# A batched matrix product on one core: the first x load divided between two issuing engines

## The chip, the core and the metric

The kernel runs on one core of a Trainium2 chip. The metric is the device time of one execution in microseconds (us); lower is better. Where a profile is quoted, its times are those of one profiled execution, counted from the start of its span. PE is TensorE, DVE is VectorE, ACT is ScalarE, POOL is GpSimd and SP is SyncE; a q behind the name (SPq) means the sequencer of that engine, which issues DMAs and waits on semaphores. Data moves between the chip's memory (HBM) and the on-chip buffers by 16 DMA engines, which all issuing engines share.

## The reference

128 independent products of a 256 x 512 matrix with a 512 x 384 matrix, all in float32:

```python
b1, b2, m, k, n = 8, 16, 256, 512, 384
x      = randn(b1, b2, m, k)      # 67.1 MB
weight = randn(b1, b2, k, n)      # 100.7 MB
out    = np.matmul(x, weight)     # 50.3 MB, float32
```

## The kernel before

**Tiling.** The 128 products are taken in 32 groups of G = 4 (the text calls a group n). A group's x is 1024 rows of 512 numbers, 2 MB: partition p holds eight rows that follow one another in memory, 16 KB (`x_sb`, two buffers). Its weights are 3 MB (`w_sb`, two buffers), and its result is 1.5 MB (`out_sb`, four slots). The first four groups and the last two load their weights in two pieces of 1.5 MB each, with 12 KB to a partition; the others in one piece with 24 KB to a partition.

**Stages of a group.** Each has T = 4 quarters.
- SyncE loads x (`load_x`, line 121) and the weights (`load_w`, line 138), and stores the result (`store`, line 160). Each load and store is one DMA, or two for weights in pieces. GpSimd makes the identity matrix for the transposes at the start, and stores one group late in the run (`store_rest`).
- VectorE casts x to bf16 (`cast_x`, line 194, four casts a group) and most of the weights (`cast_w`, line 207; `cast_short`, line 223, for the groups with divided weights). ScalarE casts the other weights (line 207).
- TensorE transposes x through PSUM (line 247), two bf16 numbers as one float32 word. ScalarE evacuates the transposed x to `x_t` (`evacuate`, line 234).
- TensorE multiplies (line 265; line 283 for the last group). ScalarE copies the products out of PSUM (`copy_out`, line 300).

**What sets the order.** The order is written out by hand: each engine has its own program (`on_sync`, `on_vector`, `on_tensor`, `on_scalar`, `on_gpsimd`), and semaphores that only count up tie them together. SyncE issues x and weights of group 0, then of group 1; x of group 2 has to wait until the four casts of group 0 have freed `x_sb0` (`x_cast`), and weights of group 2 until the weights of group 0 are cast (`w_vcast`, `w_acast`). In the loop it issues, per group, a load of x, a store of the group four before, and a load of weights. All DMAs that SyncE issues stand in one hardware queue, in that order. VectorE casts x of group 0 first, then per group its weights and x of the next group. ScalarE is one group ahead with its evacuations.

**Around the change.** SyncE's program starts with `load_x(e, 0, NG, 0)`, a DMA of 2 MB to 128 partitions that counts 16 on `x_in0` when it has landed. VectorE's first cast waits for that count. ScalarE's program starts with four increments (lines 385 to 388), which set the counters `t_copied`, `o_copied` and the two `o_out` to their starting values, and then evacuates group 0 (line 405); up to there it issues no DMA.

Of the kernel before, what the change touches and what calls it, by code (L numbers as in the profile page):

```python
# [12 lines left out]
def kernel(  # L13
# [7 lines left out]
    P = 128  # L21

    b1, b2, M, K = x.shape
# [4 lines left out]
    x_rows = x.rearrange("b1 b2 m k -> (b1 b2 m) k")  # L28
# [12 lines left out]
    G = 4  # L41
    C = P // G
    R = G * M // P
# [22 lines left out]
    def sbuf(name, shape, dtype, n):  # L66
        return [
            ctx.enter_context(nc.sbuf_tensor(f"{name}{s}", shape, dtype)) for s in range(n)
        ]
# [6 lines left out]
    def sems(name, n):  # L76
        return [tc.alloc_semaphore(f"{name}{s}") for s in range(n)]
# [3 lines left out]
    x_sb = sbuf("x_sb", [P, R, K], fp32, XS)  # L81
# [19 lines left out]
    x_in, w_in, o_out = sems("x_in", XS), sems("w_in", WS), sems("o_out", 2)  # L101
    h_in = sems("h_in", G)
    o_end = sems("o_end", 1)[0]
    rest_out = sems("rest_out", 1)[0]
    o_fin, spare = sems("o_fin", 1)[0], sems("spare", 1)[0]


# [2 lines left out]

    def load_x(e, t, U, s):
        n = t * U + s
        if not isinstance(n, int) or n >= XS:
            e.wait_ge(x_cast, n * T + (1 - XS) * T)
        rows = x_rows[bass.ds(n * (G * M), G * M)]
        if is_full(n):
            src = rows.rearrange("(i p r) k -> p i r k", i=G, p=P)
            dst = x_sb[s % XS][:].rearrange("p (i r) k -> p i r k", i=G)
        else:
            src, dst = rows.rearrange("(p r) k -> p r k", r=R), x_sb[s % XS][:]  # L120
        e.dma_start(dst, src).then_inc(x_in[s % XS], 16)  # L121

    def is_short(n):
        return isinstance(n, int) and (n < LAG or n >= NG - 2)

    def is_full(n):
        return isinstance(n, int) and n == NG - 1

    def load_w(e, t, U, s):
        n = t * U + s  # L130
        if not isinstance(n, int) or n >= WS:
            e.wait_ge(w_vcast, n * CV + (1 - WS) * CV)
            e.wait_ge(w_acast, n * CA + (1 - WS) * CA)  # L133
        d = SL // SH if is_short(n) else 1
        k = SL * KO // d
        for h in range(d):
            sem = h_in[s % WS * 2 + h] if is_short(n) else w_in[s % WS]
            e.dma_start(  # L138
                w_sb[s % WS][:, h * k : (h + 1) * k, :],
                w_rows[bass.ds(n * (G * K) + h * (G // d * K), G // d * K)].rearrange(  # L140
                    "(p k) n -> p k n", k=k
                ),
            ).then_inc(sem, 16)

    def store(e, t, U, s, pieces=1):
        n = t * U + s
        dram = o_rows[bass.ds(n * (G * M), G * M)].rearrange("(p r) n -> p r n", r=R)
        if is_full(n):
            dram = o_rows[n * G * M : (n + 1) * G * M].rearrange("(i p r) n -> p i r n", i=G, p=P)
        for q in range(pieces):  # L150
            rows = slice(q * R // pieces, (q + 1) * R // pieces)
            last = isinstance(n, int) and n >= NG - OS
            if not last and (not isinstance(n, int) or n >= 2):
                e.wait_ge(o_out[s % 2], (t * (U // 2) + s // 2) * 16 + 16)
            e.wait_ge(o_copied, n * T + ((q + 1) * T // pieces + BIAS))
            src = out_sb[:, bass.ds(slot(t, U, s) * R + q * R // pieces, R // pieces)]
            if is_full(n):
                src = src.rearrange("p (i r) n -> p i r n", i=G)
                rows = slice(0, G)
            e.dma_start(out=dram[:, rows], in_=src).then_inc(  # L160
                o_fin if last and n == NG - 1 else o_end if last else o_out[s % 2], 16
            )
# [24 lines left out]
    def cast_x(e, t, U, s, q):  # L187
        n = t * U + s
        if q == 0:
            e.wait_ge(x_in[s % XS], (t * (U // XS) + s // XS) * 16 + 16)  # L190
        e.wait_ge(t_made, n * T + (q + 1 - T + BIAS))  # L191
        rows = slice(2 * q, 2 * q + 2)
        S = SH if is_short(n) else SL
        e.tensor_copy(  # L194
            out=x_bf[s % BS][:, rows].rearrange("p r (s q c) -> p r s q c", s=S, c=KO),
            in_=x_sb[s % XS][:, rows].rearrange("p r (q s c) -> p r s q c", s=S, c=KO),
        ).then_inc(x_cast, 1)

    def cast_w(e, t, U, s, parts, first=True):
        n = t * U + s  # L200
        if first:
            e.wait_ge(p_made, n * T + (BIAS - T))
            e.wait_ge(w_in[s % WS], (t * (U // WS) + (s - LAG) // WS) * 16 + 16)  # L203
        copy = e.tensor_copy if e is nc.vector else e.copy
        for c in parts:
            i, h = c // SL, c % SL
            copy(  # L207
                out=w_bf[(s * G + i) % WBS][h * C : (h + 1) * C],
                in_=w_sb[s % WS][i * C : (i + 1) * C, h * KO : (h + 1) * KO, :],
            ).then_inc(w_vcast if c < CV else w_acast, 1)  # L210
# [17 lines left out]
    def evacuate(e, t, U, s, parts=range(T)):  # L228
        n = t * U + s
        if parts[0] == 0:  # L230
            e.wait_ge(p_made, n * T + (BIAS - T))
        for q in parts:
            e.wait_ge(t_made, n * T + (q + 1 + BIAS))
            e.copy(  # L234
                out=x_t[s % TS][:, 2 * q : 2 * q + 2],
                in_=pt[(s * T + q) % PT][:].bitcast(bf16),
            ).then_inc(t_copied, 1)
# [54 lines left out]
    def copy_out(e, t, U, s, q):  # L292
        n = t * U + s
        if q == 0:
            if isinstance(n, int) and is_shared(n - OS):
                e.wait_ge(rest_out, 16 * 3)
            elif not isinstance(n, int) or n >= OS:
                e.wait_ge(o_out[s % 2], (t * (U // 2) + s // 2) * 16 + (16 - OS // 2 * 16 + 16))
        e.wait_ge(p_made, n * T + (q + 1 + BIAS))
        e.copy(  # L300
            out=out_sb[:, bass.ds(slot(t, U, s) * R + 2 * q, 2), :],
            in_=po[(s * T + q) % PO][:, :, :N],
        ).then_inc(o_copied, 1)
# [10 lines left out]
    def on_sync(e):  # L314
        U = 2
        for n in range(LAG):
            load_x(e, 0, NG, n)
            load_w(e, 0, NG, n)
        rounds = (NG - 2 - LAG) // U
        with e.Fori(0, rounds) as t:  # L320
            for s in range(U):
                load_x(e, t, U, LAG + s)
                store(e, t, U, s)
                load_w(e, t, U, LAG + s)

        for n in range(LAG + rounds * U, NG):
            load_x(e, 0, NG, n)
            load_w(e, 0, NG, n)
        for n in range(NG - 1 - LAG, NG):
            store(e, 0, NG, n)  # L330
        e.wait_ge(o_end, 16 * (OS - 1))
        with e.Fori(0, 4):
            e.sem_inc(spare, 1)
        for _ in range(PAD):
            e.sem_inc(spare, 1)
        e.wait_ge(o_fin, 16)
# [45 lines left out]

    def on_scalar(e):
        U = 2
        e.sem_inc(t_copied, BIAS)
        e.sem_inc(o_copied, BIAS)
        for s in range(2):
            e.sem_inc(o_out[s], 16)

        def step(t, U, s):
            short = is_short(t * U + s + 1)
            evacuate(e, t, U, s + 1, range(T - 1))
            for q in range(T):
                copy_out(e, t, U, s, q)
                if q == 0:
                    evacuate(e, t, U, s + 1, range(T - 1, T))
                if q == 0 and short:
                    e.sem_inc(w_acast, CA)  # L400
                if q > 0 and not short:
                    last = CA if q == T - 1 else q
                    cast_w(e, t, U, s + 1, range(CV + q - 1, CV + last), q == 1)

        evacuate(e, 0, NG, 0)
        e.sem_inc(w_acast, CA)
        for n in range(LAG - 1):
            step(0, NG, n)
        rounds = (NG - 2 - LAG) // U
        with e.Fori(0, rounds) as t:  # L410
            for s in range(LAG - 1, LAG - 1 + U):
                step(t, U, s)
        for n in range(LAG - 1 + rounds * U, NG - 1):
            step(0, NG, n)
        for q in range(T):
            copy_out(e, 0, NG, NG - 1, q)
# [3 lines left out]
    on_vector(nc.vector)  # L420
    on_tensor(nc.tensor)
    on_scalar(nc.scalar)


# [28 lines left out]
```

## Time and profile before

| | |
|---|---|
| median of 3 runs | 515.99 us (515.84 to 516.26) |
| profiled execution | 516.01 us, of which its span is 514.2 us |
| instructions | 11664 |
| HBM read, written | 167.77 MB, 50.33 MB |
| rate over the span | 424 GB/s |
| DMA queue of SyncE (q1) | 216.54 MB, 98.8% of 16 engines' span |
| DMA queue of GpSimd (q0) | 1.57 MB, 0.7% |
| busy: PE, DVE, ACT, POOL | 62%, 77%, 80%, 1% of the span |
| the x loads | 32 of 2048 KB, median 22.3 us from issue to landing |
| the first x load | 2048 KB, issued at 0.90 us, 7.7 us from issue to landing |
| first cast of VectorE | starts at 8.65 us |
| first work of ScalarE | starts at 10.63 us |

The profile gives busy time by engine, the span in 40 equal slices (each digit is a busy share in tenths; GB/s is what the DMA engines moved), the DMA queues, the chain of work that ended last, and groups of instructions by line with what ended the idle time before them. Busy shares are averages over the whole span. The time from issue to landing of a DMA holds the time that it stands in its queue behind earlier ones. The trace behind the profile also has a record of every DMA packet, with its start, its length, its size and its queue; a packet here is one row of one partition, 16 KB of an x load, 12 or 24 KB of a weight load. A time share of the DMA engines can read a little over 1 in a narrow window, because a packet counts in the window in which it starts.

### The profile page before, as it was taken

Reading aid. Unit: us, or ns where it says so; the run is one execution under the profiler, and the core shown is the slowest. Engines: PE = TensorE matmul, PEld = TensorE weight load, DVE = VectorE, ACT = ScalarE, POOL = GpSimd, SP = SyncE. Lnnn points to the kernel's source line nnn. Section 1 sums busy time; section 2 is a strip of 40 time slices with the busy share of each in tenths; the row PEclk is TensorE's granted clock in tenths of the full one; section 3 lists DMA queues with packets and bytes.
Section 4 is the critical chain, followed back from the end, with each engine's and each line's share of the span. In section 5 each row is a group of like instructions: output and inputs, shape, how many; then the busy total and the mean of one; then the engine's idle time right before and its main releaser. Section 6 shows DMA issues by size and latency. Waiting matters only on the chain.

```text
span 514.2 us, 11664 instructions
## 1 busy us (share of the span) xinstructions
PE 316.8 (62%) x4512; PEld 222.5 (43%) x4512; DVE 397.6 (77%) x462; ACT 409.5 (80%) x387; POOL 3.7 (1%) x9
## 2 busy tenths in 40 slices
PE   2277837556675575866568656567545676474782
PEld 2255525434454343544435534345434354353551
DVE  2788757798777887778977779777798777887980
ACT  1365576997898989789978989987998798989752
POOL 0000000000000000000000000000000000010000
PEclk9687785877787778668776868886878787778887
DMA  8999999999999999999999999999999999999997
GB/s 334 429 427 422 438 423 427 436 430 435 420 427 433 433 436 429 425 429 433 440 427 428 427 435 429 438 426 426 431 437 435 425 426 429 435 435 420 422 426 308
DMA packets 15686, 218.18 MB, mean 424 GB/s; under 512 B 1728, under 2 KB 1728, under 8 KB 3008
## 3 DMA queue, kind: packets, MB, share of 16 engines
q1 hardware_dynamic: 15312, 216.54, 98.8%
q0 software_dynamic: 368, 1.57, 0.7%
q8 instruction: 3, 0.05, 0.0%
q14 instruction: 3, 0.02, 0.0%
HBM read 167.77 MB, written 50.33 MB: 424 GB/s over the span
## 4 chain that ended last, share of the span: by engine, by line
DMA 55%; DVE 31%; issue 9%; PE 1%; DVEq 1%; SPq 1%; ACT 0%; POOLq 0%
DMA w_sb<-in_weight_dram 55%; DVE w_bf L207 20%; DVE w_bf L223 5%; DVE x_bf L194 5%; PE po L283 1%; SPq L138 0%; DVEq L360 0%; SPq L121 0%; DVEq L64 0%; DVEq L203 0%; ACT out_sb L300 0%; SPq L133 0%; DVEq L191 0%; DVEq L217 0%; SPq L448 0%
## 5 line engine op out<-in xcount | busy, mean ns | idle before, releaser
L207 DVE CAST w_bf<-w_sb 32x1536 bf16<-32x1536 f32 x286 | 271.9, 951 | 81.9 <-DMA w_sb<-in_weight_dram 70.7
L265 PE MATMUL po<-w_bf,x_t 128*32 128x384 bf16 x3968 | 197.1, 358 | 34.1 <-DVE w_bf L207 29.5
L247 PE MATMUL pt<-identity,x_bf 128*128 128x128 f32 x512 | 114.7, 414 | 153.5 <-DVE x_bf L194 153.5
L207 ACT CAST w_bf<-w_sb 32x1536 bf16<-32x1536 f32 x130 | 190.9, 1468 | 5.5 <-DMA w_sb<-in_weight_dram 2.3
L247 PEld LDWEIGHTS pt<-identity,x_bf 128*128 128x128 f32 x512 | 103.4, 224 | 165.4 <-issue 165.1
L265 PEld LDWEIGHTS po<-w_bf,x_t 128*32 128x32 bf16 x3968 | 116.1, 105 | 113.8 <-issue 53.0
L300 ACT COPY out_sb<-po 128x768 f32 (+1 forms) x128 | 102.5, 801 | 58.8 <-PE po L265 54.7
L234 ACT COPY x_t<-pt 128x1024 bf16<-128x1024 bf16 x128 | 123.6, 1020 | 21.2 <-PE pt L247 20.6
L194 DVE CAST x_bf<-x_sb 128x1024 bf16<-128x1024 f32 x128 | 79.9, 688 | 12.3 <-DMA x_sb<-in_x_dram 11.5
L223 DVE CAST w_bf<-w_sb 64x1536 bf16<-64x1536 f32 x48 | 45.8, 955 | 7.4 <-DMA w_sb<-in_weight_dram 6.0
L234 ACT ACT_TABLE_LOAD x1 | 1.3, 1283 | 10.6 <-PE pt L247 10.6
L174 POOL DMA_DIRECT2D out_dram<-out_sb x3 | 3.1, 1020 | 458.9 <-DMA out_dram<-out_sb 458.9
L283 PE MATMUL po<-w_bf,x_t 128*128 128x384 bf16 x32 | 5.4, 326 | 0.4 <-DVE w_bf L223 0.4
L283 PEld LDWEIGHTS po<-w_bf,x_t 128*128 128x128 bf16 x32 | 3.1, 98 | 2.7 <-issue 0.7
masks.py:199 POOL TENSOR_SCALAR_AFFINE_SELECT identity<-identity 128x128 f32<-128x128 f32 x1 | 0.3, 283 | 0.2 <-POOL identity L306 0.2
L306 POOL MEMSET identity<- 128x128 f32 x1 | 0.2, 204 | 0.5 <-POOLq L64 0.5
L437 POOL MEMSET const-bfloat16-1.0<- 128x1 bf16 x1 | 0.1, 96 | 0.0
L437 POOL MEMSET const-uint8-127<- 128x1 uint8 x1 | 0.1, 96 | 0.0
L437 POOL MEMSET const-float32-0.0<- 128x1 f32 x1 | 0.1, 93 | 0.3 <-issue 0.3
L437 POOL MEMSET const-float32-1.0<- 128x1 f32 x1 | 0.1, 93 | 0.0
## 6 DMA issues: line engine op xcount, KB each, us to landing
w_sb<-in_weight_dram SPq DMA_DIRECT2D x26, 3072.0 KB, 18.1
x_sb<-in_x_dram SPq DMA_DIRECT2D x32, 2048.0 KB, 22.3
out_dram<-out_sb SPq DMA_DIRECT2D x31, 1536.0 KB, 25.0
w_sb<-in_weight_dram SPq DMA_DIRECT2D x12, 1536.0 KB, 16.7
out_dram<-out_sb POOLq DMA_DIRECT2D x1, 1440.0 KB, 16.8
out_dram<-out_sb POOLq DMA_DIRECT2D x1, 60.0 KB, 7.1
out_dram<-out_sb POOLq DMA_DIRECT2D x1, 36.0 KB, 17.6
```

The lines of the kernel that those rows point to most:

```text
L174: e.dma_start(out=dram[p : p + k], in_=out_sb[p : p + k, a : a + R], max_dma_last_dim=R // 2 * N * 4,).then_inc(rest_out, 16)
L194: e.tensor_copy(out=x_bf[s % BS][:, rows].rearrange("p r (s q c) -> p r s q c", s=S, c=KO), in_=x_sb[s % XS][:, rows].rearrange("p r (q s ...
L207: copy(out=w_bf[(s * G + i) % WBS][h * C : (h + 1) * C], in_=w_sb[s % WS][i * C : (i + 1) * C, h * KO : (h + 1) * KO, :],).then_inc(w_vcas ...
L223: e.tensor_copy(out=w_bf[(n * G + d * SH + a) % WBS][h * p : (h + 1) * p], in_=w_sb[n % WS][a * p : (a + 1) * p, r : r + KO, :],).then_inc ...
L234: e.copy(out=x_t[s % TS][:, 2 * q : 2 * q + 2], in_=pt[(s * T + q) % PT][:].bitcast(bf16),).then_inc(t_copied, 1)
L247: ins = e.transpose(pt[(s * T + q) % PT][:, rr, h, :], words[:, 2 * q + rr, h :: KO // 2], identity[:],)
L265: ins = e.matmul(po[(s * T + q) % PO][mine, rr, :N], x_t[s % TS][:, 2 * q + rr, ko // 2, mine, ko % 2], w_bf[(s * G + i) % WBS][:, ko, :], ...
L283: ins = e.matmul(po[(s * T + q) % PO][:, rr, :N], x_t[s % TS][:, 2 * q + rr, ko // 2, :, ko % 2], w_bf[(s * G + q) % WBS][:, ko, :], start ...
L300: e.copy(out=out_sb[:, bass.ds(slot(t, U, s) * R + 2 * q, 2), :], in_=po[(s * T + q) % PO][:, :, :N],).then_inc(o_copied, 1)
L306: e.memset(identity[:], 0.0).then_inc(id_done, 1)
L437: nc = _bacc.Bacc("TRN2", target_bir_lowering=False, num_devices=1)
```

## The change

The first load of x is divided by partitions. SyncE's DMA for group 0 now fills partitions 0 to 63 only, and counts on `x_in0` as before. ScalarE issues a DMA of its own for partitions 64 to 127, as the first instruction of its program, ahead of the four increments; it goes into ScalarE's own hardware queue and counts on a new semaphore, `x_half0`. VectorE's first cast of group 0 waits for both counts. The bytes and the layout in memory and on the chip are the same, and all later loads are as they were. In the built program ScalarE has one instruction more (the DMA), and the other engines have as many as before; VectorE's additional wait stands on a semaphore instruction that was already there.

```diff
--- before.py
+++ after.py
@@ -102,6 +102,7 @@
     h_in = sems("h_in", G)
     o_end = sems("o_end", 1)[0]
     rest_out = sems("rest_out", 1)[0]
+    x_half = sems("x_half", 1)[0]
     o_fin, spare = sems("o_fin", 1)[0], sems("spare", 1)[0]
 
 
@@ -113,12 +114,18 @@
         if not isinstance(n, int) or n >= XS:
             e.wait_ge(x_cast, n * T + (1 - XS) * T)
         rows = x_rows[bass.ds(n * (G * M), G * M)]
+        if isinstance(n, int) and n == 0:
+            return load_first(e, slice(0, P // 2), x_in[0])
         if is_full(n):
             src = rows.rearrange("(i p r) k -> p i r k", i=G, p=P)
             dst = x_sb[s % XS][:].rearrange("p (i r) k -> p i r k", i=G)
         else:
             src, dst = rows.rearrange("(p r) k -> p r k", r=R), x_sb[s % XS][:]
         e.dma_start(dst, src).then_inc(x_in[s % XS], 16)
+
+    def load_first(e, part, sem):
+        rows = x_rows[: G * M].rearrange("(p r) k -> p r k", r=R)
+        e.dma_start(x_sb[0][part], rows[part]).then_inc(sem, 16)
 
     def is_short(n):
         return isinstance(n, int) and (n < LAG or n >= NG - 2)
@@ -188,6 +195,8 @@
         n = t * U + s
         if q == 0:
             e.wait_ge(x_in[s % XS], (t * (U // XS) + s // XS) * 16 + 16)
+            if isinstance(n, int) and n == 0:
+                e.wait_ge(x_half, 16)
         e.wait_ge(t_made, n * T + (q + 1 - T + BIAS))
         rows = slice(2 * q, 2 * q + 2)
         S = SH if is_short(n) else SL
@@ -382,6 +391,7 @@
 
     def on_scalar(e):
         U = 2
+        load_first(e, slice(P // 2, P), x_half)
         e.sem_inc(t_copied, BIAS)
         e.sem_inc(o_copied, BIAS)
         for s in range(2):
```

## The prediction

> **What bounds the kernel now.** I read the page first: busy slices, the DMA queues, then the chain that ended last. After that I cut the start and the end of the span into narrow windows, and read the waits of VectorE in the first 30 us.
>
> The slices and queues on the page of the kernel before:
>
> ```profile
> DVE  2788757798777887778977779777798777887980
> ACT  1365576997898989789978989987998798989752
> DMA  8999999999999999999999999999999999999997
> GB/s 334 429 427 422 438 423 427 436 430 435 420 427 433 433 436 429 425 429 433 440 427 428 427 435 429 438 426 426 431 437 435 425 426 429 435 435 420 422 426 308
> q1 hardware_dynamic: 15312, 216.54, 98.8%
> DMA 55%; DVE 31%; issue 9%; PE 1%; DVEq 1%; SPq 1%; ACT 0%; POOLq 0%
> ```
>
> No compute engine is full in any long stretch. The 16 DMA engines are: SyncE's one queue occupies them for 98.8% of the span, and all slices but the first and the last lie between 420 and 440 GB/s. The chain's 55% on w_sb loads is mostly time in which a load stands in that queue behind others. So the time is what a pipe costs that is filled once, runs full, and is emptied once; only the first and the last slice have anything to give.
>
> Those two ends in windows (columns: stretch, its length, busy time by engine with counts, clock, DMA share, GB/s):
>
> ```profile
> 0.00:1.90 1.90, 0.00 (x0) 0.00 (x0) 0.00 (x0) 0.00 (x0) 0.69 (x6) 1.00 0.00 0
> 1.90:3.00 1.10, 0.00 (x0) 0.00 (x0) 0.00 (x0) 0.00 (x0) 0.00 (x0) 1.00 1.11 223
> 3.00:4.00 1.00, 0.00 (x0) 0.00 (x0) 0.00 (x0) 0.00 (x0) 0.00 (x0) 1.00 0.79 262
> 4.00:8.00 4.00, 0.00 (x0) 0.00 (x0) 0.00 (x0) 0.00 (x0) 0.00 (x0) 1.00 1.00 428
> ...
> 506.00:506.70 0.70, 0.00 (x0) 0.00 (x0) 0.00 (x0) 0.00 (x0) 0.00 (x0) 1.00 0.82 347
> 506.70:510.00 3.30, 0.00 (x0) 0.00 (x0) 0.00 (x0) 0.00 (x0) 0.00 (x0) 0.61 0.99 399
> 510.00:511.00 1.00, 0.00 (x0) 0.00 (x0) 0.00 (x0) 0.00 (x0) 0.00 (x0) 0.50 0.75 298
> 511.00:512.60 1.60, 0.00 (x0) 0.00 (x0) 0.00 (x0) 0.00 (x0) 0.00 (x0) 0.50 0.23 88
> 512.60:514.20 1.60, 0.00 (x0) 0.00 (x0) 0.00 (x0) 0.00 (x0) 0.00 (x0) 0.50 0.00 0
> ```
>
> The first packet starts at 1.92, 1.02 after SyncE's issue at 0.90. From 1.90 to 4.00 the engines move 223 x 1.10 + 262 x 1.00 = 507 KB, which at 428 GB/s is 1.18 us of work: the ramp wastes 2.10 - 1.18 = 0.92 us. Then the rate is full. The account closes: 218.18 MB at 428 GB/s is 509.8, and 1.90 + 0.92 + 509.8 = 512.6, where the last packet ends; 1.6 us of closing waits and barriers make 514.2. At the end most DMA engines finish by 511, a few at 511 to 512.6, so the slowest of them sets the end.
>
> How the start feeds VectorE, and what SyncE does meanwhile (start, duration, instructions, idle time before):
>
> ```profile
> 0.90 0.39 SPq L121 DMA_DIRECT2D x_sb<-in_x_dram  x1
> 1.35 0.89 SPq L138 DMA_DIRECT2D w_sb<-in_weight_dram  x2
> 2.28 0.64 SPq L121 DMA_DIRECT2D x_sb<-in_x_dram  x1
> 2.97 0.99 SPq L138 DMA_DIRECT2D w_sb<-in_weight_dram  x2
> ...
> 8.65 2.50 DVE L194 CAST x_bf<-x_sb 128x1024 bf16<-128x1024 f32 x4 [8.65 <-DMA x_sb<-in_x_dram]
> 12.41 3.91 DVE L223 CAST w_bf<-w_sb 64x1536 bf16<-64x1536 f32 x4 [1.26 <-DMA w_sb<-in_weight_dram]
> 17.22 3.91 DVE L223 CAST w_bf<-w_sb 64x1536 bf16<-64x1536 f32 x4 [0.90 <-DMA w_sb<-in_weight_dram]
> 22.13 2.50 DVE L194 CAST x_bf<-x_sb 128x1024 bf16<-128x1024 f32 x4 [0.99 <-DMA x_sb<-in_x_dram]
> 25.91 4.90 DVE L223 CAST w_bf<-w_sb 64x1536 bf16<-64x1536 f32 x5 [1.28 <-DMA w_sb<-in_weight_dram]
> ```
>
> By 3.96 SyncE has put 10.5 MB into its queue, 24.5 us of work, so the pipe can't run dry early. VectorE waits for a load four more times by 25.91, together 1.26 + 0.90 + 0.99 + 1.28 = 4.43 us.
>
> **The change part by part.** The sum is made against the profiled execution: 516.01, of which 514.2 is span and 1.8 lies around it. The median shown is 515.99, so the two stand as one.
>
> SyncE's issue of the first half. The instruction stays; it took 0.39. If its time goes with the bytes it takes about 0.20, and the six loads behind it move up to 0.19 earlier; if it goes with the number of DMA engines, nothing moves. Either way the queue already holds work when each DMA engine comes to it, so this is worth 0.
>
> ScalarE's issue. A new instruction at about 0.90, where ScalarE's first semaphore increment stands now. The nearest row is SyncE's issue at the same moment, 0.39 us. Behind it on ScalarE stand four semaphore increments (they end at 1.14 now, so 1.53 then) and the first evacuation. The increments release nobody early: TensorE's first transpose is at 9.45, the first store is issued at 37.98. ScalarE itself first has work at 10.63. Cost 0, with 8 us of cover.
>
> [...] No run shows a divided load yet.
>
> The bytes and their ends. The same 2 MB in the same 128 rows of 16 KB, 64 + 64, and 64 rows divide over 16 engines as evenly as 128. A second completion adds one 4-byte packet per DMA engine, which the packet records give as 9 ns: +0.01.
>
> VectorE's wait. One more semaphore before the first cast; a semaphore wait on VectorE is 0.02 us. What is queued behind it is all of VectorE's work, and SyncE's third x load waits for the four casts. The halves share the engines, so the later half lands about when the whole load did, 8.6. If an engine took all of SyncE's first weight piece before the second half, it would land later by 8 packets of 460 ns, 3.7 us. Less than the 4.43 us that VectorE waits anyway by 25.91; the third x load (11.18 now) has until about 27 before the queue runs dry. A later landing costs 0, an earlier one gains 0: the pipe is full.
>
> The ramp. This is the one unknown. Gain at most: 0.92, the whole waste, if two queues keep twice the reads under way while the first are slow. Loss: the packet records show the 16 DMA engines starting their first packet between 1.92 and 3.00, a spread of 1.08 within one DMA; if a second DMA's pushes come between the first's, the last engine starts up to 1.08 later. First packets took 0.61 to 1.76, later ones 0.61, so a second slow start costs one engine at most 1.15. The nearest row with two queues at once is GpSimd's store late in the run (queue q0 beside q1):
>
> ```profile
> 462.00:480.00 18.00, 10.71 (x152) 7.97 (x150) 14.51 (x17) 17.64 (x18) 1.71 (x2) 0.78 1.00 423
> 480.00:500.00 20.00, 15.46 (x277) 10.46 (x277) 18.66 (x22) 11.71 (x14) 0.00 (x0) 0.91 1.01 424
> ```
>
> With two queues 423 GB/s, with one 424, and the 16 KB packets still took 611 ns: sharing neither helps nor hurts. I take 0 for the ramp and keep -0.92 and +1.15.
>
> Sum: 0 + 0 + 0.01 + 0.02 (hidden) + 0 = 516.0. All of it is below 0.2% (1.03 us), which is about what a measurement of this kernel can tell from no change.
>
> **The rivals.**
>
> Faster: the ramp shrinks. For it: the ramp is the only idle stretch at the start, and each DMA engine would find two queues filled at once. Against it: the records show each engine working on one packet at a time, and the slow first packets end in two clusters near 3.1 and 3.7 whatever their start, as if the memory side held them. Half of the waste gives 515.5, all of it 515.1. Even that is within 0.2%; to pass 1.03 the first packets would also have to start 0.11 earlier.
>
> Slower: the two issues share one maker of descriptors. SyncE's pushes for engine after engine then alternate with ScalarE's, the spread of first starts grows from 1.08 to 2.16, and the engine that starts last is late by 1.08. As the engines run full to the end, the slowest passes that on: 517.1. It decides from 1.03 on, that is, only if nearly the whole spread doubles on the engine that also ends last. For it: SyncE's own consecutive issues are 0.45 to 0.69 apart, as if each DMA needed that long. Against it: at that pace a second DMA adds 0.45 to 0.69, which gives 516.5 to 516.7 and stays inside.
>
> The change doesn't do what it says: the first cast doesn't start earlier, since the second half ends when the whole did. The time is that of the forecast, 516.0; I expect this.
>
> **How the numbers follow.** Unmeasurable, ramp unchanged or a little off either way: 0.77, of which 0.15 is the shrunk ramp at 515.1 to 515.7. Ramp shrunk and started early, beyond 1.03: 0.07. Second DMA delaying the slowest engine by 1.03 or more, or a slow start of the new queue of that size: 0.16. Predicted 516.0. The range reaches to 515.1 (all of the ramp won) and to 517.2 (1.15 lost). Faster 0.07, same 0.77, slower 0.16.
>
> **What would show it.** In the profile after: first packet again near 1.9; a second hardware queue with 1.05 MB; 223 and 262 GB/s up to 4.00 about as now, then 428; ScalarE's issue near 0.90 at 0.39; the first cast between 8.1 and 9.2 and VectorE's next waits changed by as much; from 40 us on no difference but a shift; the last packet near 512.5. The prediction is wrong if the stretch up to 4.00 moves over 0.9 MB or under 0.1 MB, if packets beside the second queue take longer than 611 ns, or if the time between the last packet and the span's end, or around the span, grows with a second queue in use.

## The result and the profile after

The changed kernel takes 520.44 us (median of 6 runs, 520.19 to 520.59) against 515.83 us before on the same chip (515.55 to 516.26): 4.61 us more, a ratio of 1.0088 with a 95% interval of 1.0075 to 1.0101. The prediction said 516.0, with a range of 515.1 to 517.2, and no difference that can be measured. It was wrong. The profiled execution took 520.57, of which 518.8 is span, so 1.8 lies around the span, as before.

The slices and queues on the page of the changed kernel:

```profile
DMA  8999999999999999999999999999999999999997
GB/s 190 420 430 422 431 427 433 431 431 432 420 430 433 440 427 418 436 432 427 435 432 426 437 430 434 435 428 422 435 431 435 426 425 432 435 427 424 424 426 313
q1 hardware_dynamic: 15248, 215.49, 97.9%
q10 hardware_dynamic: 80, 1.05, 0.9%
```

q10 is ScalarE's queue, with the 1.05 MB that SyncE's lost. Only one of 40 slices is different in kind: the first, 190 GB/s instead of 334. The DMA digits look the same as before, 8 and then 9. So the DMA engines were as *occupied* as before in that slice, and moved little more than half as much.

The start and the end in narrow windows (stretch, its length, busy time by engine, clock, DMA share, GB/s):

```profile
0.00:1.90 1.90, 0.00 (x0) 0.00 (x0) 0.00 (x0) 0.00 (x0) 0.68 (x6) 1.00 0.00 0
1.90:3.00 1.10, 0.00 (x0) 0.00 (x0) 0.00 (x0) 0.00 (x0) 0.00 (x0) 1.00 0.85 238
3.00:4.00 1.00, 0.00 (x0) 0.00 (x0) 0.00 (x0) 0.00 (x0) 0.00 (x0) 1.00 1.16 262
4.00:8.00 4.00, 0.00 (x0) 0.00 (x0) 0.00 (x0) 0.00 (x0) 0.00 (x0) 1.00 0.96 201
8.00:12.00 4.00, 0.00 (x0) 0.00 (x0) 0.00 (x0) 0.00 (x0) 0.00 (x0) 1.00 1.01 208
...
20.00:462.00 442.00, 282.88 (x4032) 196.69 (x4032) 354.17 (x411) 367.38 (x346) 0.00 (x0) 0.78 1.01 430
...
516.00:517.20 1.20, 0.00 (x0) 0.00 (x0) 0.00 (x0) 0.00 (x0) 0.00 (x0) 0.50 0.20 76
517.20:518.80 1.60, 0.00 (x0) 0.00 (x0) 0.00 (x0) 0.00 (x0) 0.00 (x0) 0.50 0.00 0
```

Up to 4.00 nothing stands out: 524 KB moved, against 507 KB before. Then, from 4 to 12 us, where the kernel before moved 428 and 427 GB/s, this one moves 201 and 208, at a DMA share of 0.96 and 1.01. The second of these windows in the kernel before:

```profile
8.00:12.00 4.00, 2.55 (x12) 2.58 (x13) 2.50 (x4) 1.36 (x2) 0.00 (x0) 1.00 1.00 427
```

The loss is (428 - 205) x 8.0 = 1.8 MB, or 4.2 us at 428 GB/s. After 20 us the rate is the old one, and the closing 1.6 us are the same as before.

How the issues and VectorE stand (start, duration, instruction, idle time before it):

```profile
0.90 0.58 SPq L128 DMA_DIRECT2D x_sb<-in_x_dram  x1
1.54 1.29 SPq L145 DMA_DIRECT2D w_sb<-in_weight_dram  x2
...
0.90 0.55 ACTq L128 DMA_DIRECT2D x_sb<-in_x_dram  x1
...
13.18 2.50 DVE L203 CAST x_bf<-x_sb 128x1024 bf16<-128x1024 f32 x4 [13.18 <-DMA x_sb<-in_x_dram]
16.91 3.91 DVE L232 CAST w_bf<-w_sb 64x1536 bf16<-64x1536 f32 x4 [1.23 <-DMA w_sb<-in_weight_dram]
21.86 3.91 DVE L232 CAST w_bf<-w_sb 64x1536 bf16<-64x1536 f32 x4 [1.03 <-DMA w_sb<-in_weight_dram]
26.60 2.50 DVE L203 CAST x_bf<-x_sb 128x1024 bf16<-128x1024 f32 x4 [0.84 <-DMA x_sb<-in_x_dram]
```

ScalarE did issue at 0.90, beside SyncE. The first cast starts at 13.18 instead of 8.65, 4.53 later. VectorE's next waits are about as long as they were (1.23, 1.03, 0.84 against 1.26, 0.90, 0.99): the whole stream of loads is late, not just the first, so these waits hide nothing.

The packet records of the trace say why 4 to 12 us is slow. Before, each DMA engine took its first 16 KB packet in 0.61 to 1.76 us and the other seven of the first load in 0.61 to 0.64 each, but for five packets of the second round (up to 1.37). Now the first take 0.75 to 1.22, the second 1.00 to 1.26, and the six others 1.16 to 1.30, through both halves; their median is 1.28. ScalarE's four packets went first on every engine, then SyncE's four. Counting bytes, the stream is behind that of the kernel before by 0.28 us at 0.5 MB, 1.6 at 1 MB, 4.2 at 2 MB (the end of the load), 4.5 at 5 MB, and 4.5 when the last packet ends. All of the loss arises in this one load and in the weight packets that start while its last ones finish, and none of it is given back.

### The profile page after: what moved, and what is told of

It reads as the page before. It is cut to its first block, busy times and chain, and to the rows that moved or that the text cites. A ratio compares the mean times of both kernels' runs of the same rounds, so it can differ in the third digit from the quotient of the medians.

```text
span 518.8 us, 11665 instructions
## 1 busy us (share of the span) xinstructions
PE 321.1 (62%) x4512; PEld 223.9 (43%) x4512; DVE 397.6 (77%) x462; ACT 409.4 (79%) x387; POOL 3.8 (1%) x9
## 3 DMA queue, kind: packets, MB, share of 16 engines
q10 hardware_dynamic: 80, 1.05, 0.9%
## 4 chain that ended last, share of the span: by engine, by line
DMA 52%; DVE 31%; issue 10%; PE 3%; ACT 1%; DVEq 1%; SPq 1%; ACTq 0%; POOLq 0%
DMA w_sb<-in_weight_dram 52%; DVE w_bf L216 20%; DVE x_bf L203 5%; DVE w_bf L232 5%; PE po L274 2%; PE po L292 1%; ACT w_bf L216 1%; SPq L145 0%; ACT out_sb L309 0%; DVEq L369 0%; ACT x_t L243 0%; DVEq L64 0%; DVEq L212 0%; SPq L128 0%; SPq L124 0%
## 5 line engine op out<-in xcount | busy, mean ns | idle before, releaser
L274 PE MATMUL po<-w_bf,x_t 128*32 128x384 bf16 x3968 | 201.5, 365 | 33.2 <-DVE w_bf L216 20.4
L274 PEld LDWEIGHTS po<-w_bf,x_t 128*32 128x32 bf16 x3968 | 117.8, 107 | 115.6 <-issue 50.6
```

What stands on the lines that cost most here:

```text
L274: ins = e.matmul(po[(s * T + q) % PO][mine, rr, :N], x_t[s % TS][:, 2 * q + rr, ko // 2, mine, ko % 2], w_bf[(s * G + i) % WBS][:, ko, :], ...
```

## The experiments

The theory I formed from these records, called P below: a DMA that reaches only one half of the partitions is written at half the rate, whoever issues it. Its rivals: two queues filled at once slow each other (Q); a DMA of 64 partitions is slow as such (S); the reading side is slow, since the change reads 1 MB in one piece per DMA (H). All diffs are against the changed kernel and show the lines that matter; all ratios are against runs of the kernel before on the same chip, each with its 95% interval.

**Both halves from SyncE, no second queue.**

```diff
-            return load_first(e, slice(0, P // 2), x_in[0])
+            load_first(e, slice(0, P // 2), x_in[0])
+            return load_first(e, slice(P // 2, P), x_half)
...
-        load_first(e, slice(P // 2, P), x_half)
```

> SyncE issues both halves, partitions 0 to 63 and then 64 to 127, one behind the other in its own queue; ScalarE issues nothing and has no queue. Theory P (partitions: a DMA that reaches only one half of the partitions is written at half the rate, whoever issues it): x packets of 1.28 us again, first cast near 13, 519.8 to 520.8. Theory Q (two queues filled at once slow each other at the start): one queue, packets of 0.61 us, 515.5 to 516.3. [...]

Measured: 520.54 us, ratio 1.0091 (1.0074 to 1.0108). Its windows:

```profile
4.00:8.00 4.00, 0.00 (x0) 0.00 (x0) 0.00 (x0) 0.00 (x0) 0.00 (x0) 1.00 0.94 197
8.00:12.00 4.00, 0.00 (x0) 0.00 (x0) 0.00 (x0) 0.00 (x0) 0.00 (x0) 1.00 0.97 200
```

The whole loss without ScalarE's issue, and packets of 1.28 us again. Q falls: the second queue isn't the cause.

**Even partitions from SyncE, odd ones from ScalarE.**

```diff
-            return load_first(e, slice(0, P // 2), x_in[0])
+            return load_first(e, slice(0, P, 2), x_in[0])
...
-        load_first(e, slice(P // 2, P), x_half)
+        load_first(e, slice(1, P, 2), x_half)
```

> As in the change, but SyncE loads the even partitions and ScalarE the odd ones: two queues, 64 partitions and four packets of 16 KB to a DMA engine in each, but each DMA spread over all the partitions. P: no half is left out, packets of 0.61 us after the first, 515.4 to 516.4. Q, and theory S (a DMA of 64 partitions is slow as such): 519.8 to 520.8.

Measured: 516.17 us, ratio 1.0008 (0.9998 to 1.0017).

```profile
4.00:8.00 4.00, 0.00 (x0) 0.00 (x0) 0.00 (x0) 0.00 (x0) 0.00 (x0) 1.00 0.96 408
8.00:12.00 4.00, 2.23 (x11) 2.26 (x12) 2.50 (x4) 1.04 (x1) 0.00 (x0) 1.00 1.03 437
```

As many partitions, bytes, packets and queues as in the change; only which partitions a DMA holds, and which addresses it reads for them, is different. ScalarE's packets again go first on nearly every engine, and packets take 0.61 us. The loss is gone, and S with it. The even rows are also read from addresses twice as far apart, so H was still open; the next two runs part it from P.

**The spread partitions fed from one piece of memory, and the halves fed from spread rows.** Both put group 0's x rows in another order on the chip, so that its products belong to other rows and its results are not the reference's; the work is the same.

```diff
-            return load_first(e, slice(0, P // 2), x_in[0])
+            return load_first(e, slice(0, P, 2), slice(0, P // 2), x_in[0])
...
-    def load_first(e, part, sem):
+    def load_first(e, part, block, sem):
...
-        e.dma_start(x_sb[0][part], rows[part]).then_inc(sem, 16)
+        e.dma_start(x_sb[0][part], rows[block]).then_inc(sem, 16)
...
-        load_first(e, slice(P // 2, P), x_half)
+        load_first(e, slice(1, P, 2), slice(P // 2, P), x_half)
```

> Even partitions from SyncE and odd ones from ScalarE, as in the run before, but read from memory as the change reads: SyncE's DMA takes the first 1 MB in one piece, ScalarE's the second. (Group 0 gets its x rows in another order, so its products belong to other rows; the work is the same.) P: 515.4 to 516.4. Theory H (the reading side: 1 MB in one piece to 16 DMA engines is what was slow): 519.8 to 520.8.

The second has the two slices of each call exchanged:

```diff
-            return load_first(e, slice(0, P // 2), x_in[0])
+            return load_first(e, slice(0, P // 2), slice(0, P, 2), x_in[0])
...
-        load_first(e, slice(P // 2, P), x_half)
+        load_first(e, slice(P // 2, P), slice(1, P, 2), x_half)
```

> Partitions 0 to 63 from SyncE and 64 to 127 from ScalarE as in the change, but SyncE's DMA reads the even 16 KB rows of the 2 MB and ScalarE's the odd ones, so that each DMA engine reads from addresses as far apart as before the change. (Group 0 gets its x rows in another order; the work is the same.) P: packets of 1.28 us, 519.8 to 520.8. H: 515.4 to 516.4.

Measured: 516.07 us, ratio 1.0005 (0.9996 to 1.0015), for spread partitions; 520.78 us, ratio 1.0098 (1.0081 to 1.0115), for halves. The windows of the first, then of the second:

```profile
4.00:8.00 4.00, 0.00 (x0) 0.00 (x0) 0.00 (x0) 0.00 (x0) 0.00 (x0) 1.00 0.97 412
8.00:12.00 4.00, 2.64 (x13) 2.67 (x14) 2.50 (x4) 1.44 (x2) 0.00 (x0) 1.00 1.00 427
```

```profile
4.00:8.00 4.00, 0.00 (x0) 0.00 (x0) 0.00 (x0) 0.00 (x0) 0.00 (x0) 1.00 0.93 197
8.00:12.00 4.00, 0.00 (x0) 0.00 (x0) 0.00 (x0) 0.00 (x0) 0.00 (x0) 1.00 0.96 197
```

The four ways to pair a side of reading with a side of writing are now all measured, and the time goes with the partitions alone. H falls.

**Divided by rows instead of partitions, still between SyncE and ScalarE.**

```diff
-        e.dma_start(x_sb[0][part], rows[part]).then_inc(sem, 16)
+        e.dma_start(x_sb[0][:, part], rows[:, part]).then_inc(sem, 16)
...
-            return load_first(e, slice(0, P // 2), x_in[0])
+            return load_first(e, slice(0, R // 2), x_in[0])
...
-        load_first(e, slice(P // 2, P), x_half)
+        load_first(e, slice(R // 2, R), x_half)
```

> The first x load divided by rows instead: SyncE loads the first four of each partition's eight rows, ScalarE the last four, both to all 128 partitions, in pieces of 8 KB. Two queues as in the change. P: each DMA reaches all partitions, packets of about 0.31 us for 8 KB, 515.5 to 516.4. That the order of the queues (ScalarE's four packets first, then SyncE's) costs by itself: 517 or more.

Measured: 515.74 us beside 515.75 before, ratio 1.0003 (0.9993 to 1.0012); 8 KB packets of 0.31 us.

```profile
1.90:3.00 1.10, 0.00 (x0) 0.00 (x0) 0.00 (x0) 0.00 (x0) 0.00 (x0) 1.00 1.08 179
3.00:4.00 1.00, 0.00 (x0) 0.00 (x0) 0.00 (x0) 0.00 (x0) 0.00 (x0) 1.00 0.76 279
4.00:8.00 4.00, 0.00 (x0) 0.00 (x0) 0.00 (x0) 0.00 (x0) 0.00 (x0) 1.00 1.03 434
```

This is the change without its defect: two issuers, all partitions in each. It gains nothing either. By 4.00 it has moved 179 x 1.10 + 279 = 476 KB, against 507 before (a packet counts where it starts, so this is rough). A second issuer doesn't shorten the ramp.

**Sixteen, then 32 neighbouring partitions to a DMA, then every fourth partition.** SyncE issues all of them. The last two were planned after the result of the first; their diffs show only what they put in place of the added lines of the first.

```diff
-            return load_first(e, slice(0, P // 2), x_in[0])
+            for c in range(0, P, 16):
+                load_first(e, slice(c, c + 16), x_in[0] if c == 0 else x_half)
+            return
...
-                e.wait_ge(x_half, 16)
+                e.wait_ge(x_half, 7 * 16)
...
-        load_first(e, slice(P // 2, P), x_half)
```

> SyncE loads the first x in eight DMAs of 16 neighbouring partitions, one packet of 16 KB to a DMA engine in each. [...] P with halves alone (only the halves 0 to 63 and 64 to 127 differ): packets of 1.28 us, 520 to 521.5.

```diff
+            for c in range(0, P, 32):
+                load_first(e, slice(c, c + 32), x_in[0] if c == 0 else x_half)
...
+                e.wait_ge(x_half, 3 * 16)
```

> SyncE loads the first x in four DMAs of 32 neighbouring partitions, two packets to a DMA engine in each. [...] That the rate goes with the number of neighbouring partitions (64 took 1.28 us a packet, 16 took 2.23): about 1.7 us a packet, 8 x 1.1 longer, 523 to 526.

```diff
+            for c in range(4):
+                load_first(e, slice(c, P, 4), x_in[0] if c == 0 else x_half)
...
+                e.wait_ge(x_half, 3 * 16)
```

> Four DMAs from SyncE again, each to 32 partitions, but to every fourth one (0, 4, 8 ...; 1, 5, 9 ...). [...] That small DMAs, or four issues in a row, cost the time: about that of the four DMAs of 32 neighbours.

Measured: 528.11 us, ratio 1.024 (1.0218 to 1.0262), for 16 neighbours; 520.25, ratio 1.0088 (1.0071 to 1.0105), for 32 neighbours; 516.00, ratio 1.0003 (0.9994 to 1.0013), for every fourth. Windows of the three in this order:

```profile
4.00:8.00 4.00, 0.00 (x0) 0.00 (x0) 0.00 (x0) 0.00 (x0) 0.00 (x0) 1.00 0.99 115
8.00:12.00 4.00, 0.00 (x0) 0.00 (x0) 0.00 (x0) 0.00 (x0) 0.00 (x0) 1.00 0.89 102
```

```profile
4.00:8.00 4.00, 0.00 (x0) 0.00 (x0) 0.00 (x0) 0.00 (x0) 0.00 (x0) 1.00 1.11 234
8.00:12.00 4.00, 0.00 (x0) 0.00 (x0) 0.00 (x0) 0.00 (x0) 0.00 (x0) 1.00 0.96 196
```

```profile
4.00:8.00 4.00, 0.00 (x0) 0.00 (x0) 0.00 (x0) 0.00 (x0) 0.00 (x0) 1.00 0.95 356
8.00:12.00 4.00, 1.28 (x6) 1.31 (x7) 2.07 (x4) 0.09 (x1) 0.00 (x0) 1.00 1.01 419
```

With 16 neighbours a 16 KB packet takes 2.23 us, and the load is about a quarter as fast (102 to 115 GB/s against 428). With 32 neighbours it takes 1.28, the same as with 64: the rate doesn't go with the number of partitions. With 32 spread partitions it takes 0.61 mostly (0.74 in the seventh round), the same as with 128. At half the rate a packet would take 1.22 us, two times 0.61, and at a quarter 2.44; the halves and the 32 neighbours took 1.28, at 197 to 208 and 196 to 234 GB/s, and the 16 neighbours 2.23. So the time goes with which partitions a DMA holds, and not with the two halves alone: 32 or 64 neighbours are slow, as many spread partitions are not, and 16 neighbours are slower still. Why that is so no run shows.

The packets in their order show a little more. With 32 neighbours, the fifth packets (in order of their starts, sixteen to a round), the first that go to partitions 64 to 95 while others still finish 32 to 63, took 1.13 to 1.19 us. The third (first to 32 to 63) and the seventh (first to 96 to 127) took 1.27 to 1.28, with no such dip. It is as if 0 to 31 and 32 to 63 held each other up, and the two sides of 64 did so less.

The price for sixteens, 12.4 us, is less than that of eight packets of four times 0.61 on each engine, 8 x (2.44 - 0.61) = 14.6 by estimate: packets took 2.23 us and not four times 0.61, and the first packet of each engine only 0.99 to 1.45.

**The second load divided, the first left whole; all from SyncE.**

```diff
-        if isinstance(n, int) and n == 0:
-            return load_first(e, slice(0, P // 2), x_in[0])
+        if isinstance(n, int) and n == 1:
+            load_second(e, slice(0, P // 2), x_in[1])
+            return load_second(e, slice(P // 2, P), x_half)
...
-            if isinstance(n, int) and n == 0:
+            if isinstance(n, int) and n == 1:
                 e.wait_ge(x_half, 16)
...
-        load_first(e, slice(P // 2, P), x_half)
```

`load_second` is `load_first` for group 1: the next 1024 rows of x, into `x_sb[1]`.

> The first x load is whole again, from SyncE alone; the second one (group 1), which stands behind 5 MB in the queue, is divided by partition halves, both issued by SyncE. P: the halves take 8 x 0.67 = 5.4 us longer wherever they stand, less what the DMA engines gain by being out of step; the engines have no slack, 519.5 to 521. That the price is one of the start (slow first packets, an empty pipe): 515.5 to 516.3.

Measured: 521.10 us, ratio 1.0106 (1.0088 to 1.0124), 5.35 more than before, and 0.1 above the range that P gave. The window in which the second load runs, in this kernel, and then the same window in the kernel before:

```profile
15.00:25.00 10.00, 0.00 (x0) 0.00 (x0) 5.28 (x6) 0.85 (x1) 0.00 (x0) 1.00 1.02 224
```

```profile
15.00:25.00 10.00, 2.04 (x10) 2.05 (x11) 7.61 (x10) 1.50 (x2) 0.00 (x0) 0.55 1.00 424
```

The price isn't one of the start. It is even larger than in the three kernels with halves in the first load (4.6 to 5.0). The packet records show where: the first two packets of an engine together took 0.9 us longer than undivided here, and 0.05 longer in the changed kernel, since those of the first load are slow anyway.

**The whole first load from ScalarE.**

```diff
-            return load_first(e, slice(0, P // 2), x_in[0])
+            return
...
-            if isinstance(n, int) and n == 0:
-                e.wait_ge(x_half, 16)
...
-        load_first(e, slice(P // 2, P), x_half)
+        load_first(e, slice(0, P), x_in[0])
```

> The first x load is whole, to all 128 partitions, but ScalarE issues it from its own queue as its first act, and SyncE starts with the first weights. It measures the second queue without the division. P: 515.4 to 516.3. A second queue in use costs something by itself (at its start, or around the span): 516.3 to 517.

Measured: 516.49 us, ratio 1.0015 (1.0005 to 1.0024), 0.7 more than before. P's range missed it; it lies in that of a second queue that costs something by itself.

```profile
4.00:8.00 4.00, 0.00 (x0) 0.00 (x0) 0.00 (x0) 0.00 (x0) 0.00 (x0) 1.00 0.98 421
8.00:12.00 4.00, 0.00 (x0) 0.00 (x0) 0.00 (x0) 0.00 (x0) 0.00 (x0) 1.00 1.04 445
...
13.09 2.50 DVE L201 CAST x_bf<-x_sb 128x1024 bf16<-128x1024 f32 x4 [13.09 <-DMA x_sb<-in_x_dram]
15.50 7.85 DVE L230 CAST w_bf<-w_sb 64x1536 bf16<-64x1536 f32 x8
23.38 2.50 DVE L201 CAST x_bf<-x_sb 128x1024 bf16<-128x1024 f32 x4
26.69 3.91 DVE L230 CAST w_bf<-w_sb 64x1536 bf16<-64x1536 f32 x4 [0.81 <-DMA w_sb<-in_weight_dram]
```

This run is worth more than its purpose. x and the first weights share the DMA engines here, so the first cast starts at 13.09, as late as in the changed kernel (13.18). Yet the time grows by 0.7 and not by 4.6. The cover works: VectorE finds its weights already there (no wait before 15.50), and catches up: its casts of group 1's weights start at 26.69 instead of 25.91. So a late first cast explains at most 0.7 of the 4.6 us. The rest is the price of bytes that weren't moved.

Where the 0.7 comes from stays open. Divided by rows, a second queue cost nothing that can be measured. In the profiled execution here the stream is at most 0.2 us late over its first 20 MB. It is 0.7 late at 25 MB, after 16 KB packets of up to 1.43 us between 55 and 58 us, about 0.3 late from 60 to 200 MB, and its last packet ends 0.82 late.

## Why the prediction was wrong, step by step

- *The kernel is bound by the 16 DMA engines, filled once, run full, emptied once.* Right, and it is why the loss comes through undiminished: 4.5 us by 5 MB, 4.5 at the last packet.
- *SyncE's and ScalarE's issues.* Each was priced at 0.39 at most and costed at nothing. They took 0.58 and 0.55, longer than the 0.39 for all of the rows, and the first packet started at 2.27 instead of 1.92. With even and odd partitions the issues were as slow and the first packet as late (2.24), and the time was within its error of before. Right that they are hidden.
- *The bytes and their ends.* **This is the step that failed.** It argued that 64 rows divide over 16 DMA engines as evenly as 128, left the packet at 611 ns, and put the term at 0.01 us. Evenness over the engines that *move* the data says nothing about the partitions that *receive* it. Measured: 1.28 us a packet (median) from the third on. Six such packets on each engine were together 3.9 us longer than before. The rest of the 4.5 is the later start, 0.2 on the average engine, and the first weight packet, which took 0.74 to 0.95 us instead of 0.46 beside the last x packets. So the later half did not land "about when the whole load did": the first cast started 4.53 later.
- *The ramp is the one unknown, 0 from the row of GpSimd's store.* The row was the wrong neighbour. It has two queues, but 1440 of its 1536 KB go through a DMA of 120 partitions, and it is a store, so it could not show what a load to half of the partitions costs. I looked for the nearest row by the number of queues, and the change differed in something else as well. The ramp itself lost 0.28 us by 0.5 MB, inside its bounds; divided by rows, it didn't change. The 0.92 of waste was too small a reading: it counts a packet's bytes where the packet starts. Spread over the packets' time, the ramp before cost 1.1 us.
- *VectorE's wait is covered by 4.43 us of other waits.* Right as a mechanism: with the whole load from ScalarE, a first cast 4.44 later cost 0.7 at most. It didn't help, because the landing was late together with everything behind it.
- *The slower rival, a shared maker of descriptors that spreads the first packets.* Wrong: first packets started within 0.36 us of one another (2.27 to 2.62), before within 1.08. The 0.16 for a slower kernel stood on this and on a slow start of the new queue, and neither is what happened.
- *What would show the prediction wrong* named packets of over 611 ns beside a second queue. The packets did show it, but for a reason that needs no second queue.

Left open: why ScalarE's packets went ahead of SyncE's on each engine. With halves running in turn, each had only its own partitions to write; had the engines worked on both at once, less might have been lost. The fifth packets speak for it: they are the first of the second half, run while other engines finish the first, and took 1.16 to 1.20 us instead of 1.28. Divided by rows, the two queues' packets did alternate. No run forced the order.

## What to carry to other kernels

Ask of a DMA which partitions it reaches, not only how many bytes and engines it has: here a load to partitions 0 to 63 or 64 to 127 ran at half the rate (197 to 208 GB/s from 4 to 12 us, against 428), one to 16 neighbours at about a quarter (102 to 115), but 32 or 64 spread over the whole range at about the full rate (356 to 437). (64 neighbours on both sides of 64, as 32 to 95, were not tried.) If a load has to be divided, divide it by rows inside the partitions (ratio 1.0003 here), or by every second partition (1.0008). And where the DMA engines are the bound, look at GB/s beside their busy share: a share near 1 at half the usual rate says that each packet takes twice as long (here 0.96 at 201 GB/s, with packets of 1.28 us for 0.61). Which side holds it up, the exchanged rows decided here.

## What the runs showed that I had not expected

- A DMA to 64 partitions took longer to issue than one to 128: 0.55 to 0.58 us against 0.39, whether neighbours or every second one, and its first packet started 0.31 to 0.37 later. DMAs of 16 or 32 neighbours took 0.40 to 0.42 each, those of every fourth partition 0.57 to 0.59. The cause wasn't looked for.
- In the changed kernel the page's DMA share and digits do not betray the fault at all; only the GB/s of the first slice does (190 for 334).
- Two halves one behind the other get little back from DMA engines that are out of step: in the second load 14 of the 16 engines started within 0.41 us of one another and the last about 1.6 us after the first. The packets around the change of halves were shorter, mostly 1.07 to 1.16 us; after the first, nearly all others took 1.2 to 1.3.
